# NSA units that hold one branch of two heads, and output projections that begin inside the attention, in a two-layer hybrid-attention kernel

## The chip, the cores and the metric

The kernel runs on one core of one Trainium2 chip. The metric is the device time of one execution in microseconds (us), the median of the runs shown. Engines are named as the profile names them: PE is TensorE's matmul, PEld its weight load, DVE is VectorE, ACT ScalarE, POOL GpSimd, SP SyncE (here the queue that issues the weight DMAs).

## What is computed

A forward pass over 256 tokens of width 1024 through two layers in fp32. Each layer is: half a SwiGLU feed-forward block, a mixer, half a feed-forward block, each with a norm that is scaled and shifted by a conditioning vector, and gated into the residual. Layer 0's mixer is the even one, layer 1's the odd one. Cut to what matters here:

```python
def even_mixer(y, ...):
    # 8 MLA heads: causal softmax attention, q and k of 96 columns, v of 64
    o_a = mla_mixer(...)
    # 8 NSA heads in 2 groups; k and v are shared by the 4 heads of a group
    o_b = gt[0] * o_c + gt[1] * o_s + gt[2] * o_w   # compressed, selected, window branch
    return concat([o_a, o_b]) @ w_out               # [256, 1024] @ [1024, 1024]

def odd_mixer(y, ...):
    o_c = dilated_mixer(...)    # 4 slots, each one softmax over 3 groups of heads
    o_d = moba_mixer(...)       # 4 heads
    return concat([o_c, o_d]) @ w_out               # [256, 512] @ [512, 1024]
```

With 256 tokens the selected branch covers every block and the window covers every key, so both are a causal softmax over 256 keys with a bias, each with its own k, v and gate. The compressed branch is 15 keys a head.

## The kernel before

**Exact products.** A dense product with weights is done as three fp32r matmuls of 512 columns (`mm3`, lines 198 to 200): high part times high part, high times the weights' low part, low times high. Each weight piece of 128 x 1024 therefore is prepared first: `prep` copies the DMA's slot to H on ACT (line 161) and, deferred, subtracts it to L on DVE (line 166). At most four pieces are prepared ahead (`HLN`); `piece(i)` hands out the i-th of them and issues subtractions still owed, `settle` issues all that are owed, `pop` gives the first one back and prepares the next. Slots come by SP's queue, eight at a time, and the next DMA is issued when a slot is done with.

**Attention.** `attention` runs over units in a software pipeline; each engine gets its instructions in the order of the code. In step i (lag 2), with `fill(i)` at its end:

```python
s3(i - 3)        # even i: values of a pair of units, PE L1107, into one PSUM bank o
turns(i - 2)     # probabilities transposed, PE L1080
s0(i + 2)        # scores, PE L1025 and L1026, then warm[i + 2] warming products, PE L479
scale(i - 1)     # DVE L1067 to L1072
logits(i + 1)    # bias, mask and row minimum, DVE L1037 and L1039
exps(i)          # ACT L1052
s4()             # o split in a high and a low part, ACT L832 and DVE L833
out_of(i - 2)    # the transposes copied to PT, ACT L1090 (a third branch: DVE L1088)
settle(); fill(i)
```

The even mixer has 16 units: 0 to 7 are the MLA heads, 8 to 15 the NSA heads, one unit a head, in the order (p, g) with head 4g + p. An NSA unit has two branches, selected and window. q and k of group g lie in partitions 64g to 64g + 63, so both branches of a unit use the same half of the partitions for their scores, which have 64 rows. `s3` takes two units and writes their 64 output columns to the two halves of o; it goes over branches, then over key tiles z, then over the two units. For NSA the pair starts with one product for the compressed branch (`extra`, PE L1553). `WKE` and `WKO` give the warming products of each unit in the even and the odd attention; a warming product is a matmul of the identity whose result is not used. `fill` runs background work: two products of the next conditioning vector (DVE L497), in steps 1 to 9 the compressed branch's chain, and from step 13 on `prep(True)` for the first pieces of the output projection. The odd mixer has 8 units, even ones with three branches in one softmax, odd ones with one.

**PSUM.** Two tags with four banks each: `acc` for transposes, o and projections, `wps` for scores and the transposes of the next norm.

**Output projection.** `out_proj` runs behind the attention and a flush of the background work: 8 pieces j times 2 token tiles t times 6 products in the even mixer, 4 pieces in the odd one. `oT` holds the rows of the MLA heads (j 0 to 3), `o2` those of the NSA heads (j 4 to 7). Behind tile 0's last product the residual and the norm of tile 0 (`blk.res(0)`) run on DVE and ACT while PE does tile 1; then `blk.tr(0)` transposes tile 0 for the next feed-forward block (PE L695).

Of the kernel before, what the change touches and what calls it, by code (L numbers as in the profile page):

```python
# [27 lines left out]
HLN = 4  # L28
# [8 lines left out]
def kernel(  # L37
# [572 lines left out]
    WKO = 4, 0, 0, 6, 2, 4, 2, 4  # L610
    WKE = 2, 1, 2, 2, 2, 2, 2, 2, 1, 1, 2, 2, 2, 1, 1, 1
# [402 lines left out]
    def attention(ap, units, stile, lag, fill, warm):  # L1014

        n = len(units)
        nbmax = max(len(u["br"]) for u in units)
        st = {}

        def s0(i):  # L1020
            u = units[i]
            st[i] = []
            for qT, kT, _, _ in u["br"]:
                ps = wps()
# [68 lines left out]
        def s3(i):  # L1093
            pair = [(units[j], st.pop(j), j % 2) for j in (i - 1, i)]
            o = acc()
# [4 lines left out]
            for b in range(nbmax):  # L1100
                for z in range(2):
                    for u, pt, hp in pair:
                        nb = len(u["br"])
                        if b >= nb:
                            continue
                        v = u["br"][b][3]
                        T.matmul(o[64 * hp:64 * hp + 64, 128 * z:256], lhsT=v[z], rhs=pt[:, b, 256 * z:256 + 128 * z],  # L1107
                                 start=first and b == 0 and z == 0, stop=b == nb - 1 and z == 1,
                                 skip_group_check=True)
# [33 lines left out]
    def out_proj(oT, nj, n):  # L1143
        o = [[acc(), acc()] for _ in range(2)]
        blk = Block(o, n)

        def mm(t, j, h, l, qr=(0, 1)):
            tsl = slice(128 * t, 128 * t + 128)
            sh, sl = oT(j)
            for q in qr:  # L1150
                qs = slice(512 * q, 512 * q + 512)
                mm3(o[t][q], sh[:, tsl], sl[:, tsl], h[:, qs], l[:, qs], j == 0, j == nj - 1)

        for j in range(nj - HLN):
            for t in range(2):
                mm(t, j, *piece(0))
            pop()
        for t in range(2):
            for j in range(HLN - QM):
                mm(t, nj - HLN + j, *piece(0 if t else j))  # L1160
                if t:
                    pop(later=True)
            for q in range(2):
                for j in range(QM):
                    mm(t, nj - QM + j, *piece((0 if q else j) if t else HLN - QM + j), qr=(q,))
                    if t and j < QM - 1 and q:
                        pop(later=True)
            if t:
                settle(LS)
                blk.tr(0)  # L1170
                pop(later=True)
# [780 lines left out]
```

## Time and profile before

| what | value |
|---|---|
| median of 3 runs | 1102.04 us (1101.65 to 1104.19) |
| profiled execution, its own time | 1103.17 us |
| span of the profiled execution | 1101.4 us |
| mean granted PE clock | 0.987 of full |
| PE busy | 1049.4 us, 95% of the span |
| DVE busy | 828.2 us, 75% |
| ACT busy | 533.5 us, 48% |
| DMA | 250.77 MB, 228 GB/s over the span |

The times in the rows are from the span's start. The even mixer's attention starts its first scores at 306.8 us and its last values end at 370.7; its projection ends at 392.9. The odd attention's first scores start at 855.4, and its projection runs from 890.8 to 902.0. A busy share is an average over all stages; what a change in one stage is worth is read from the stage itself, from the waits that end last there. Matmuls are pipelined, so their own durations are longer than the distance from one to the next.

### The profile page before, as it was taken

What the parts mean: (1) busy time and instruction counts of PE and PEld (TensorE: products, weight loads), DVE (VectorE), ACT (ScalarE), POOL (GpSimd) and SP (SyncE); (2) the same over time, 40 slices, a digit from 0 to 9 for tenths busy, and PEclk for the clock granted to TensorE, in tenths of its full rate; (3) what the DMA queues carried; (4) which work ended last, traced back from release to release, by engine and by line L of the source; (5) the groups of instructions that cost most, each with busy time, mean ns of one, the idle gap of its engine ahead of it and who ended that gap; (6) DMA issues with size and microseconds to landing.
All of it is one profiled execution on the core that took longest, in us unless ns stands there. A gap on an engine that the chain in (4) does not pass through costs nothing.

```text
span 1101.4 us, 14077 instructions
## 1 busy us (share of the span) xinstructions
PE 1049.4 (95%) x5031; PEld 847.6 (77%) x5031; DVE 828.2 (75%) x1430; ACT 533.5 (48%) x913; POOL 45.9 (4%) x93
## 2 busy tenths in 40 slices
PE   6899999997989989999999999999999999999998
PEld 5678778876677768888887888888688777888886
DVE  5779877769788488997757999864779868666653
ACT  4444434554348466444446544433645666444441
POOL 3000020003400000000000000000000000000000
PEclk9999999999989999999999999999999999999999
DMA  9999998747690357999863899884278517765500
GB/s 335 306 364 339 317 347 258 259 142 248 224 243 2 115 177 244 353 363 304 269 209 115 270 357 344 283 286 151 77 253 244 153 39 262 234 229 191 164 1 38
DMA packets 169818, 250.77 MB, mean 228 GB/s; under 512 B 10741, under 2 KB 111559, under 8 KB 169748
## 3 DMA queue, kind: packets, MB, share of 16 engines
q1 hardware_dynamic: 166736, 248.35, 68.8%
q0 software_dynamic: 2576, 1.39, 0.9%
q8 instruction: 39, 0.64, 0.3%
q14 instruction: 31, 0.25, 0.1%
q10 hardware_dynamic: 436, 0.13, 0.0%
HBM read 247.59 MB, written 2.23 MB: 227 GB/s over the span
## 4 chain that ended last, share of the span: by engine, by line
PE 79%; DVE 10%; ACT 4%; DMA 3%; issue 2%; SPq 1%; POOL 0%; ACTq 0%; DVEq 0%
PE wps L198 13%; PE wps L200 13%; PE wps L199 13%; PE acc L198 10%; PE acc L200 10%; PE acc L199 10%; DVE L L166 3%; DMA slot<-in_ada_w_dram 2%; PE wps L880 2%; DVE ada L497 2%; PE acc L1107 1%; ACT xn L1052 1%; ACT H L161 1%; DMA slot<-in_ffn_w_in_dram 1%; SPq L95 1%
## 5 line engine op out<-in xcount | busy, mean ns | idle before, releaser
L166 DVE TENSOR_TENSOR L<-slot,H 128x1024 fp32r<-128x1024 f32 (+4 forms) x316 | 376.7, 1200 | 136.3 <-ACT H L161 128.5
L161 ACT ACTIVATE H<-slot 128x1024 fp32r<-128x1024 f32 (+4 forms) x316 | 325.7, 1040 | 280.5 <-PE acc L200 134.5
L198 PE MATMUL wps<-H,y 128*128 128x512 f32 (+1 forms) x736 | 290.2, 394 | 1.7 <-ACT y L714 1.6
L199 PE MATMUL wps<-L,y 128*128 128x512 f32 (+1 forms) x736 | 285.2, 387 | 6.3 <-DVE L L166 4.6
L200 PE MATMUL wps<-H,y 128*128 128x512 f32 (+1 forms) x736 | 284.8, 387 | 0.0
L199 PEld LDWEIGHTS wps<-L,y 128*128 128x128 f32 x736 | 139.2, 189 | 36.2 <-DVE L L166 10.9
L198 PEld LDWEIGHTS wps<-H,y 128*128 128x128 f32 x736 | 139.1, 189 | 28.8 <-ACT y L714 1.8
L200 PEld LDWEIGHTS wps<-H,y 128*128 128x128 f32 x736 | 138.8, 189 | 28.4 <-DVE y L720 0.9
L198 PE MATMUL acc<-H,gT 128*128 128x512 f32 x352 | 142.5, 405 | 1.0 <-DVE g L868 1.0
L200 PE MATMUL acc<-H,gT 128*128 128x512 f32 x352 | 138.5, 393 | 0.0
L199 PE MATMUL acc<-L,gT 128*128 128x512 f32 x352 | 138.2, 393 | 0.0
L497 DVE SCALAR_TENSOR_TENSOR ada<-slot,c,ada 128x512 f32<-128x512 f32 x155 | 116.3, 751 | 2.9
L198 PEld LDWEIGHTS acc<-H,gT 128*128 128x128 f32 x352 | 66.0, 188 | 24.7 <-issue 11.0
L200 PEld LDWEIGHTS acc<-H,gT 128*128 128x128 f32 x352 | 66.0, 188 | 15.4
L497 DVE SCALAR_TENSOR_TENSOR ada<-slot,cact,ada 128x512 f32<-128x512 f32 x96 | 72.1, 751 | 5.6 <-DMA slot<-in_ada_w_dram 3.8
L199 PEld LDWEIGHTS acc<-L,gT 128*128 128x128 f32 x352 | 66.1, 188 | 13.3
L832 ACT ACTIVATE gT<-wps 128x512 fp32r<-128x512 f32 (+2 forms) x53 | 26.5, 501 | 94.6 <-PE wps L880 90.5
L866 ACT ACTIVATE s<-wps 128x256 f32<-128x256 f32 (+1 forms) x86 | 31.9, 377 | 47.0 <-PE wps L200 46.4
L198 PE MATMUL acc<-H,y 128*128 128x512 f32 (+2 forms) x128 | 50.1, 392 | 2.2 <-ACT H L161 1.1
L199 PE MATMUL acc<-L,y 128*128 128x512 f32 (+2 forms) x128 | 49.4, 386 | 2.7 <-DVE L L166 2.7
L833 DVE TENSOR_TENSOR gT<-wps,gT 128x512 fp32r<-128x512 f32 (+2 forms) x53 | 30.1, 568 | 27.6 <-ACT gT L832 26.8
L200 PE MATMUL acc<-H,y 128*128 128x512 f32 (+2 forms) x128 | 49.2, 384 | 0.1
(333 smaller groups left out, 1037.4 us busy)
## 6 DMA issues: line engine op xcount, KB each, us to landing
slot<-in_ffn_w_in_dram SPq DMA_DIRECT2D x160, 512.0 KB, 6.3
slot<-in_ffn_w_out_dram SPq DMA_DIRECT2D x40, 1024.0 KB, 7.0
slot<-in_ada_w_dram SPq DMA_DIRECT2D x160, 256.0 KB, 5.4
slot<-in_ada_w_dram SPq DMA_DIRECT2D x24, 1024.0 KB, 7.3
slot<-in_od_w_in_dram SPq DMA_DIRECT2D x12, 1024.0 KB, 5.2
slot<-in_ada_w_dram SPq DMA_DIRECT2D x16, 512.0 KB, 9.6
slot<-in_ffn_w_in_dram SPq DMA_DIRECT2D x16, 384.0 KB, 4.3
slot<-in_nsa_cmp_w_dram SPq DMA_DIRECT2D x4, 1024.0 KB, 9.2
```

What stands on the lines that cost most here:

```text
L95: nc.sync.dma_start(view(t), src)
L161: A.activation(hv, w, AF.Copy)
L166: eng.tensor_tensor(lv, w, hv.bitcast(F32), op=OP.subtract)
L198: T.matmul(o, lhsT=sh, rhs=wh, start=start, stop=False)
L199: T.matmul(o, lhsT=sh, rhs=wl, start=False, stop=False)
L200: T.matmul(o, lhsT=sl, rhs=wh, start=False, stop=stop)
L497: V.scalar_tensor_tensor(a, w[:, j], c[:, j:j + 1], a, op0=OP.mult, op1=OP.add)
L832: A.activation(dst[0], src, AF.Copy)
L833: V.tensor_tensor(dst[1], src, dst[0].bitcast(F32), op=OP.subtract)
L866: A.activation(s[:, 0:m], ab[t][:, 0:m], AF.Silu)
L880: T.transpose(ps[0:mm, 256 * ft + 128 * t:256 * ft + 128 * t + 128], st[u, t][:, 128 * ft:128 * ft + mm], ident)
L1052: A.activation(s[b][:, c0:c1], s[b][:, c0:c1], AF.Exp, scale=-1.0, bias=nm[:, b, q:q + 1], accum_out=den[:, b, q:q + 1])
```

## The change

NSA units are regrouped: a unit is now one branch b of the two heads p and 4 + p, of which one lies in partitions 0 to 63 and the other in 64 to 127. A pair of units still holds the same two heads and both branches. `s3` then goes over the pair's first unit and its second unit one after another, and alternates between the two heads inside a unit.

`out_proj` becomes a class. `begin` swaps the two PSUM tags, so that the projection's four accumulators take the banks of the scores, and `some` issues blocks (t, j) of 6 products in `fill`: in the even attention 8 of 16 blocks in steps 14 to 18 (`EF`), in the odd one 3 of 8 in steps 7 to 9 (`OF`). `end` issues the rest in the order of before. Pieces 0 to 3 of the even projection are given back inside the attention, and each time the next one is prepared; the first preparation moves from step 13 to step 12. The warming products are fewer: MLA units have 1 each (15 before, 8 now), NSA units none (11 before), the last two odd units none (6 before).

```diff
+    sets = ["a", "w"]
+    def bank_of(tag):
+        return psum.tile([128, 512], F32, tag=tag, name={"a": "acc", "w": "wps"}[tag])
     def acc():
-        return psum.tile([128, 512], F32, tag="acc", name="acc")
+        return bank_of(sets[0])
     def wps():
-        return psum.tile([128, 512], F32, tag="w", name="wps")
+        return bank_of(sets[1])
...
-    WKO = 4, 0, 0, 6, 2, 4, 2, 4
-    WKE = 2, 1, 2, 2, 2, 2, 2, 2, 1, 1, 2, 2, 2, 1, 1, 1
+    WKO = 4, 0, 0, 6, 2, 4, 0, 0
+    WKE = 1, 1, 1, 1, 1, 1, 1, 1, 0, 0, 0, 0, 0, 0, 0, 0
+    EF = {14: ((0, 0),), 15: ((1, 0), (0, 1)), 16: ((1, 1), (0, 2)), 17: ((1, 2), (0, 3)), 18: ((1, 3),)}
+    OF = {7: ((0, 0),), 8: ((0, 1),), 9: ((0, 2),)}
...
+        mine, scores = [lambda tag=tag: bank_of(tag) for tag in sets]
...
             for qT, kT, _, _ in u["br"]:
-                ps = wps()
+                ps = scores()
...
-                ps = acc()
+                ps = mine()
...
-            for b in range(nbmax):
+            if "both" in units[i]:
+                steps = [(u, pt, b, b, j == 0, j == 1) for u, pt, j in pair for b in range(2)]
+                steps = [steps[0:2], steps[2:4]]
+            else:
+                steps = [[(u, pt, b, hp, b == 0, b == len(u["br"]) - 1) for u, pt, hp in pair if b < len(u["br"])]
+                         for b in range(nbmax)]
+            for group in steps:
                 for z in range(2):
-                    for u, pt, hp in pair:
-                        nb = len(u["br"])
-                        if b >= nb:
-                            continue
+                    for u, pt, b, hp, begin, end in group:
                         v = u["br"][b][3]
                         T.matmul(o[64 * hp:64 * hp + 64, 128 * z:256], lhsT=v[z], rhs=pt[:, b, 256 * z:256 + 128 * z],
...
-    def out_proj(oT, nj, n):
-        o = [[acc(), acc()] for _ in range(2)]
-        blk = Block(o, n)
...
+    class OutProj:
+        def begin(self):
+            sets.reverse()
+            self.o = [[acc(), acc()] for _ in range(2)]
...
+        def some(self, *tj):
+            for t, j in tj:
+                gone = sum((z, i) in self.made for i in range(self.nj - HLN) for z in (1,))
+                self.mm(t, j, *piece(j - gone))
+                self.made.add((t, j))
+                if t and j < self.nj - HLN:
+                    pop(later=True)
+
+        def end(self):
+            nj, made = self.nj, self.made
+            blk = Block(self.o, self.n)
+            self.some(*[(t, j) for j in range(nj - HLN) for t in range(2) if (t, j) not in made])
+            for t in range(2):
+                for j in range(HLN - QM):
+                    if (t, nj - HLN + j) not in made:
+                        self.mm(t, nj - HLN + j, *piece(0 if t else j))
+                    if t:
+                        pop(later=True)
...
-                    if i >= 13:
+                    if i >= 12:
                         prep(True)
+                    if i == 14:
+                        proj_out.begin()
+                    proj_out.some(*EF.get(i, ()))
...
-                def mk2(p, g):
-                    h = 4 * g + p
-
+                def mk2(p, b):
...
-                    gs = slice(64 * g, 64 * g + 64)
-                    return dict(br=[(qT[gs, p, :], kT[gs, b, :], ba[:, h, :],
-                                     [vn[t][:, b, 64 * g:64 * g + 64] for t in range(2)]) for b in range(2)],
-                                extra=extra_, gate=gv[:, h, 1:3, :], dst=lambda: dst2(p))
+                    br = []
+                    for g in range(2):
+                        gs = slice(64 * g, 64 * g + 64)
+                        br.append((qT[gs, p, :], kT[gs, b, :], ba[:, 4 * g + p, :],
+                                   [vn[t][:, b, 64 * g:64 * g + 64] for t in range(2)]))
+                    return dict(br=br, both=True, extra=extra_, gate=gv[:, p:8:4, 1 + b, :], dst=lambda: dst2(p))
...
-                attention(e2, units + [mk2(p, g) for p in range(4) for g in range(2)], ring, 2, fill, WKE)
+                proj_out = OutProj(lambda j: (oT[:, j, 0], oT[:, j, 1]) if j < 4 else
+                                   (o2[0][:, j - 4, 0], o2[0][:, j - 4, 1]), 8, 1)
+                attention(e2, units + [mk2(p, b) for p in range(4) for b in range(2)], ring, 2, fill, WKE)
                 bg_flush()
...
+                return proj_out.end()
...
                     bg(QA[i])
+                    if i == 6:
+                        proj_out.begin()
+                    proj_out.some(*OF.get(i, ()))
+
+                proj_out = OutProj(lambda j: (oT[:, j, 0], oT[:, j, 1]), 4, 4)
                 attention(o2, units, ring, 2, fill, WKO)
```

## Rows read from the trace of the kernel before

**Rows 1.** The page, part 4: the shares of the chain that ended last, by engine.

```profile
PE 79%; DVE 10%; ACT 4%; DMA 3%; issue 2%; SPq 1%; POOL 0%; ACTq 0%; DVEq 0%
```

**Rows 2.** Windows: the busy time of each engine by stage. Columns: stretch in us, its length, busy time and instructions of PE, PEld, DVE, ACT and POOL, the granted PE clock, the DMA engines' busy share, GB/s. The stages are the half-clock stretch of the MLA units, two NSA stretches, the end of the even attention, its projection, the end of the odd attention, its projection.

```profile
316.30:324.40 8.10, 8.10 (x43) 7.09 (x43) 4.77 (x19) 3.92 (x14) 1.01 (x2) 0.62 1.13 258
...
332.50:345.40 12.90, 12.90 (x83) 9.64 (x83) 12.39 (x63) 10.23 (x39) 0.00 (x0) 1.00 0.00 1
345.40:357.28 11.88, 11.88 (x80) 8.72 (x80) 9.92 (x57) 10.07 (x38) 0.00 (x0) 1.00 0.01 2
357.28:370.70 13.42, 11.59 (x77) 7.74 (x77) 8.23 (x20) 9.57 (x27) 0.00 (x0) 0.87 0.26 79
370.70:392.94 22.24, 22.24 (x98) 18.21 (x99) 11.06 (x19) 8.58 (x12) 0.00 (x0) 1.00 0.43 142
...
877.40:890.78 13.38, 11.90 (x84) 8.39 (x84) 9.12 (x36) 7.66 (x26) 0.00 (x0) 1.00 0.21 78
890.78:901.98 11.20, 11.20 (x50) 8.98 (x50) 6.09 (x15) 4.61 (x8) 0.00 (x0) 1.00 0.01 2
```

**Rows 3.** The chain that ended last, in order of time, in the NSA steps of the even attention. Columns: start us, us, engine, output, line, how many instructions (a matmul of fp32 operands is two).

```profile
346.43 0.64 PE wps L479 x4
...
350.09 1.45 PE acc L1107 x16
351.54 0.81 PE acc L1080 x6
352.34 0.41 PE wps L1025 x2
352.76 0.43 PE wps L1026 x2
353.19 0.22 PE wps L1025 x2
353.41 0.43 PE wps L1026 x2
353.85 0.42 PE wps L479 x2
354.27 0.66 PE acc L1080 x6
...
356.84 0.43 PE acc L1553 x2
```

**Rows 4.** All waits of DVE from 324 to 357.3 us (us in total, times, longest), and the row of the timeline with the longer one (idle time before it and what ended it in brackets).

```profile
DVE yb L833 <- ACT yb L832: 1.6, 1, 1.6
DVE qTn L828 <- PE acc L1444: 0.7, 1, 0.7
...
352.00 0.42 DVE L833 TENSOR_TENSOR yb<-acc,yb 128x256 fp32r<-128x256 f32 x1 [1.63 <-ACT yb L832]
```

**Rows 5.** The timeline of ACT in steps 12 and 13: the split of a pair, the two PT copies of unit 11 and the first H copy of the projection's pieces.

```profile
351.58 0.39 ACT L832 ACTIVATE yb<-acc 128x256 fp32r<-128x256 f32 x1 [1.48 <-PE acc L1107]
...
354.69 0.87 ACT L1090 ACTIVATE PT<-acc 128x384 f32<-128x384 f32 x2
...
355.45 1.06 ACT L161 ACTIVATE H<-slot 128x1024 fp32r<-128x1024 f32 x1
```

**Rows 6.** The chain again, at the end of the even attention and where the next stage's transposes begin.

```profile
361.12 1.74 ACT xn L1052 x8
362.86 0.38 ACT PT L1090
...
363.29 2.72 PE acc L1107 x11
...
392.94 0.89 PE wps L695 x8
```

**Rows 7.** Windows again, columns as in rows 2: stretches around the two falls of the PE clock in the even attention, and a stretch of the odd attention with little PE work.

```profile
314.00:316.30 2.30, 0.00 (x1) 0.01 (x1) 2.16 (x7) 0.00 (x0) 0.54 (x1) 0.86 1.09 346
...
316.00:318.00 2.00, 1.70 (x7) 1.52 (x8) 1.93 (x5) 0.81 (x3) 1.01 (x2) 0.50 1.09 348
...
359.22:363.29 4.07, 2.29 (x14) 1.20 (x12) 4.00 (x10) 3.99 (x13) 0.00 (x0) 1.00 0.01 2
...
364.00:366.00 2.00, 2.00 (x12) 1.20 (x9) 0.54 (x3) 0.56 (x1) 0.00 (x0) 0.50 0.73 173
...
880.60:884.39 3.79, 2.31 (x15) 1.45 (x14) 3.27 (x14) 3.79 (x17) 0.00 (x0) 1.00 0.55 199
```

**Rows 8.** The chain at the end of the odd attention, and from the timeline there a joint pair's values and the transposes of unit 5.

```profile
882.07 0.27 ACT oTo L832
...
883.97 0.38 ACT PT L1090
...
886.13 1.66 PE acc L1080 x12
...
890.11 0.66 PE wps L583 x2
...
901.98 0.89 PE wps L695 x8
...
878.50 2.16 PE L1107 MATMUL acc<-PT,vt 128*64 128x256 f32 x16
...
882.77 0.55 PE L1080 MATMUL acc<-cp,xn 128*128 128x128 f32 x3 [0.98 <-ACT PT L1090]
```

More of the change, by code (lines that the diff above doesn't have):

```diff
@@ L1094, in s3 @@
             pair = [(units[j], st.pop(j), j % 2) for j in (i - 1, i)]
-            o = acc()
+            o = mine()
             first = True
@@ L1099, in s3 @@
                 first = False
-            for b in range(nbmax):
+            if "both" in units[i]:
[5 more added lines that the diff above has]
+            for group in steps:
                 for z in range(2):
-                    for u, pt, hp in pair:
-                        nb = len(u["br"])
-                        if b >= nb:
-                            continue
+                    for u, pt, b, hp, begin, end in group:
                         v = u["br"][b][3]
                         T.matmul(o[64 * hp:64 * hp + 64, 128 * z:256], lhsT=v[z], rhs=pt[:, b, 256 * z:256 + 128 * z],
-                                 start=first and b == 0 and z == 0, stop=b == nb - 1 and z == 1,
-                                 skip_group_check=True)
+                                 start=first and begin and z == 0, stop=end and z == 1, skip_group_check=True)
             st["o"] = (units[i]["dst"], o)
@@ L1150, in mm @@
             for q in qr:
                 qs = slice(512 * q, 512 * q + 512)
-                mm3(o[t][q], sh[:, tsl], sl[:, tsl], h[:, qs], l[:, qs], j == 0, j == nj - 1)
-        for j in range(nj - HLN):
-            for t in range(2):
[L1156 to L1160, printed above, removed]
+                mm3(self.o[t][q], sh[:, tsl], sl[:, tsl], h[:, qs], l[:, qs], j == 0, j == self.nj - 1)
@@ new lines, in some @@
+        def some(self, *tj):
[9 more added lines that the diff above has]
+            self.some(*[(t, j) for j in range(nj - HLN) for t in range(2) if (t, j) not in made])
+            for t in range(2):
+                for j in range(HLN - QM):
[3 more added lines that the diff above has]
+                        pop(later=True)
+                for q in range(2):
+                    for j in range(QM):
+                        if (t, nj - QM + j) not in made:
+                            self.mm(t, nj - QM + j, *piece((0 if q else j) if t else HLN - QM + j), qr=(q,))
+                        if t and j < QM - 1 and q:
+                            pop(later=True)
@@ L1161, in out_proj @@
                 if t:
+                    settle(LS)
+                    blk.tr(0)
                     pop(later=True)
[L1163 to L1171, printed above, removed]
-            else:
-                blk.res(0)
@@ L1174, in out_proj @@
-        return blk
+                else:
+                    blk.res(0)
+            return blk
     def load_bias(dst, b0, eng):
```

11 lines of the change are left out of this document (6 added, 5 removed).

## The prediction, made blind

> **What bounds the kernel now.** I read the page first: the chain that ended last is 79% TensorE [rows 1], and nearly all of it is the dense products of lines 198 to 200, which the change moves but does not thin. So only the two attention stages and the products right behind them can move. I then read the windows by stage [rows 2]. The reader is to see that TensorE is busy without a gap in both NSA stretches and in both projections, that the two stretches in which it is not, 357.28 to 370.70 and 877.40 to 890.78, are the ends of the two attentions, and that DMA stands still from 332.5 to 357.28, so no transfer is late there.
>
> Next the chain through the NSA steps [rows 3]: every link is TensorE, one step's scores 0.41 + 0.43 + 0.22 + 0.43 = 1.49 us, warming products 0.42 (one) or 0.64 (two), six transposes 0.66 to 0.81, the compressed branch's product 0.43, the values 1.45. But VectorE is as tight: between 324 and 357.3 it waits twice only, 0.7 us on the copy of q and 1.63 us at 352.00 on the split of a finished pair [rows 4]. So from 324.4 to 350.4 a faster TensorE buys nothing, and what it can buy first is that 1.63 us. ScalarE comes third: 1.74 us of exponentials, 0.87 for two PT copies, 0.39 for the split, 1.06 for each H copy [rows 5, 6].
>
> The end of the even attention is read from the same chain [rows 6]: the exponentials and a PT copy on ScalarE hold TensorE until 363.29, and then the values take 2.72 us for 11 passes. [...]
>
> **Scores in two halves.** The values show how halves behave: 16 passes in 1.45 us [rows 3]. At 0.215 a pass of 256 columns and 0.11 of 128 they would be 8 x 0.215 + 8 x 0.11 = 2.6 us one after another, so two output halves run at once. For scores the order in the queue stays head 0 (128, 256 columns), head 1 (128, 256). If matmuls start in order, head 1's first passes can begin only beside the last 256-column pass of head 0, which saves 0.22 a unit. Bounds: 0 if row halves don't overlap, 0.65 if a whole head disappears. I take 0.22, since the values' passes too overlap in order: 8 units, 1.8 us of TensorE.
>
> **Warming products.** Each costs 0.22 (0.64 less 0.42). NSA units lose 11 (2.4 us), MLA units 7 (1.5 us), odd units 6 (1.3 us). In the odd attention and behind 324.4 in the even one they are hidden: ScalarE and VectorE carry the odd chain until 884.35 [rows 8], VectorE the even one until 350.4. Two MLA units lie in 316.3 to 324.4, where the clock is 0.62 and TensorE is busy all 8.10 us [rows 2] and ahead of VectorE's 0.7 us wait; one product there is 0.43 at the low clock, one 0.22: I take 0.5 us, bounds 0 and 0.65.
>
> The rows show the clock low after 2.30 us with no matmul (314 to 316.3, then 0.50), but full through 2.31 busy of 3.79 us in the odd attention [rows 7]. With 4.2 us taken from the 24.8 us between 332.5 and 357.28, TensorE still works for 20.6 of them, so I count no loss. [...]
>
> **Order of the values.** A unit now holds one branch of two heads, so the first half of a pair's values (0.73 of 1.45) needs only the first unit's PT; before, each branch alternated between both units. That half runs ahead of the wait.
>
> **Preparation one step earlier.** H copy and L subtraction of weight piece 0 move from step 13 to step 12, and pieces 4 to 7 from the projection into steps 15 to 18. VectorE has room for the L's: 8.23 busy of 13.42 us at the end [rows 2]. ScalarE gets 1.06 more before unit 11's PT. No DMA is added; the slots only come free earlier, and the queues are empty then.
>
> **The even sum.** Unit 11's PT was ready at 354.69 + 0.87 = 355.56 [rows 5]. It moves by -0.5 (MLA), -1.63 (VectorE's wait, since values of units 8 and 9 now start on their PT and not behind 2.4 + 1.8 us of scores and warming), +1.06 (H copy): 354.5. With 0.73 of the values ahead of it, TensorE's list starts as if at 353.8 where it started at 357.28. From there it has no gaps. A block is 6 products: 96 took 22.24 us (98 records in that window, two of them the next stage's) [rows 2], so 0.232 each and 1.39 a block. The list, with 0.2 for each drain between products and narrower passes not yet in the rows (two of them):
> three pairs of values 3 x 1.45; two compressed products 2 x 0.63 with their drain; four sets of transposes 0.81 + 0.66 + 0.81 + 0.66; eight blocks 11.1; the 48 products left 11.1; drains 0.4. Sum 4.35 + 1.26 + 2.94 + 11.1 + 11.1 + 0.4 = 31.2, so the next stage's transposes start at 385.0 and not at 392.94 [rows 6]: 7.9 us gained.
> Does anything else bind? ScalarE from 354.5 to unit 13's PT: H 1.06, exponentials 1.74, split 0.39, PT 0.87, H 1.06, exponentials 1.74, PT 0.87 = 7.7, at 362.2. TensorE needs that PT at 353.8 + 1.45 + 0.81 + 1.39 + 0.66 + 2.78 + 0.63 + 0.73 = 362.25. They meet; if ScalarE is later, the blocks' cover is gone and each us there costs one. Banks: the blocks' four were the score banks, free after unit 15's logits, which is before 357.28 less the shift.
>
> **The odd sum.** The wait before unit 5's transposes is for a bank that the split of the pair before frees, behind the exponentials [rows 8]: not touched. Block 1 runs 883.3 to 884.7, where unit 5's PT came at 884.35; then values 2.1, twelve transposes 1.66, two blocks 2.8, values 2.1, the gate's product 0.66, 30 products at 0.233 = 7.0: 901.1, where the transposes started at 901.98 [rows 8]. Gain 0.9; bounds -0.6 (three more drains) and 2.0 (all of TensorE's idle time there: 13.38 less 11.90 [rows 2], and the rest of the warming).
>
> **Sum.** 7.9 + 0.9 = 8.8 us. The profiled execution has a span of 1101.4 and took 1103.17; less 8.8 it is 1094.4. The median of the three runs is 1102.04, 1.13 below it: 1093.2.
>
> **Rivals.**
> 1. Only the gaps at the ends are filled; the start of the list stays at 357.28 because VectorE or ScalarE, saturated in the steps before, don't let it move. Then 392.94 - 357.28 = 35.66 against 31.2: 4.5, plus 0.9: 1096.6. For it: ScalarE was busy 10.07 of 11.88 us in 345.4 to 357.28 [rows 2] and gets an H copy more. Against: VectorE's 1.63 us wait is real, and it waited for TensorE.
> 2. The clock falls in the NSA steps, for want of warming products, and the kernel is slower. [...] For it: the fall at 364 came in the same stage. Against: the odd row named above.
> 3. The change doesn't do what it says: the blocks stand in TensorE's queue ahead of transposes and values that ScalarE waits for, and stretch the attention by what they take off the projection. Then the gain is the idle time that remains, near 0: 1102. Against: in steps 16 to 18 no exponentials are left, so little waits.
> 4. All of TensorE's savings count, as if VectorE were not tight: 4.2 + 0.65 + 0.73 before the list, then 4.5 and 2.0: 12.1 us, 1089.9. Against: VectorE's two waits sum to 2.3 us.
>
> **How the numbers follow.** Forecast (gains 6 to 11 us) 0.63, rival 1 (3.5 to 6) 0.18, rival 3 0.08, rival 2 0.07, rival 4 0.04. The measurement can tell about 0.3%, 3.3 us. Faster: 0.63 + 0.18 + 0.04 = 0.85; same 0.08; slower 0.07. The range goes from rival 4 to the weakest of rival 1 (a gain of 3.5): 1090 to 1098.5, which leaves out 0.15 above and a little below; the forecast's own range is 1091 to 1096.
>
> **What would show it.** Right: L479 gone from the NSA steps; unit scores at 1.27 and not 1.49; VectorE's wait on the pair of units 8 and 9 under 0.5 us; lines 198 to 200 between the transposes from about 357 on, with the clock at 1.00; the next transposes (L695) near 385 and 8.8 us earlier after the odd stage. Wrong: a clock under 0.9 between 330 and 370; TensorE waiting for PT between blocks; a second wait of VectorE of over 1 us; FFN stages of another length than before.

## The result, and the profile after

The changed kernel took 1093.65 us (median of 8 runs, 1090.37 to 1096.28) where the kernel before took 1103.24 on the same chip (8 runs): a ratio of 0.9913, interval 0.9895 to 0.9931. That is 9.6 us faster; the forecast was 1093.2 us, 8.8 us below before. The profiled execution of after has a span of 1092.4 and took 1094.18, 9.0 us less than that of before on either count.

Five marks split both spans into stages: the first transposes of the MLA heads, the first product with the compressed keys (kcT), the next stage's transposes behind the even projection, the copy of k at the start of the odd attention, and the next transposes behind the odd projection.

| stretch, us | before | after | less | forecast |
|---|---|---|---|---|
| start to MLA transposes | 302.95 | 303.64 | -0.69 | 0 |
| MLA units, to kcT | 26.40 | 26.19 | 0.21 | 0.5 |
| NSA units and even projection | 63.43 | 53.89 | 9.54 | 7.4 |
| feed-forward stages, to copy of k | 464.50 | 464.47 | 0.03 | 0 |
| odd attention and projection | 44.54 | 44.71 | -0.17 | 0.9 |
| rest | 199.58 | 199.50 | 0.08 | 0 |

So that the total came out near the forecast is in part luck, out of errors that cancel: the even stage (MLA, NSA and projection) gave 9.75 for 7.9, the odd one, in this execution, nothing for 0.9, and the stages ahead took 0.69 longer.

The page of after, parts 1 and 4: busy times, and the chain by engine (before: [rows 1]).

```profile
PE 1038.4 (95%) x4983; PEld 837.6 (77%) x4983; DVE 827.3 (76%) x1430; ACT 532.5 (49%) x913; POOL 45.9 (4%) x93
...
PE 76%; DVE 13%; ACT 4%; DMA 4%; issue 2%; POOL 0%; SPq 0%; ACTq 0%; DVEq 0%
```

TensorE lost 3% of the chain, VectorE gained 3: the NSA steps are no longer a chain of TensorE links [rows 3] but of VectorE's, up to 351.2. Windows of after: MLA units, NSA units up to the gapless list, that list, and the odd stage (columns as in [rows 2]).

```profile
303.64:329.83 26.19, 22.06 (x143) 18.76 (x142) 21.93 (x76) 13.18 (x42) 2.07 (x4) 0.87 1.02 253
329.83:353.34 23.51, 23.48 (x172) 15.82 (x172) 22.67 (x120) 19.81 (x74) 0.00 (x0) 1.00 0.01 3
353.34:383.72 30.38, 30.29 (x169) 23.81 (x166) 21.09 (x53) 18.84 (x43) 0.00 (x0) 1.00 0.44 139
848.19:892.90 44.71, 41.42 (x248) 31.68 (x247) 31.82 (x127) 26.91 (x91) 0.00 (x0) 0.96 0.38 111
```

The list of TensorE work is whole (30.29 us busy of 30.38) and at a clock of 1.00 from 353.34 on; below full clock are the MLA units (0.87) and the odd stage (0.96). The chain of after at the start and end of the list:

```profile
350.50 0.34 DVE xn L1049
350.85 0.34 DVE yb L841
351.28 1.84 ACT xn L1062 x8
353.12 0.38 ACT PT L1100
353.55 1.24 PE acc L1120 x7
354.79 0.81 PE acc L1090 x6
355.60 0.23 PE wps L204
...
383.88 0.89 PE acc L703 x8
```

The seven records at 353.55 are the second half of a pair's values; the first half ran ahead of the wait, so the list counts from 354.79 - 1.45 = 353.34. From there to 383.88 it has no gap: 30.54 us, where before took 35.66 from 357.28 to 392.94.

Scores on TensorE, from the timeline of after. The queue holds head 0 (128 columns, 256), then head 1 (128, 256).

```profile
349.43 0.50 PE L1035 MATMUL wps<-kTn,qTn 64*128 64x128 f32 x4
349.75 0.61 PE L1036 MATMUL wps<-kTn,qTn 64*128 64x256 f32 x4
350.29 0.88 PE L1090 MATMUL acc<-cp,xn 128*128 128x128 f32 x6
```

Both heads' 128-column passes are recorded ahead of both heads' 256-column ones (the four records of the first start by 349.7, the first of the others at 349.75), and the four products of a unit are over in 350.29 - 349.43 = 0.86 us, against 1.49 [rows 3]. Five of the eight NSA units show this; in the other three the second head starts later and the unit takes 1.30 to 1.65 us up to the next instruction.

### The profile page after: what moved, and what is told of

It is laid out like the page before. It is cut to its first block, busy times and chain, and to the rows that moved or that the text cites. A ratio compares the mean times of both kernels' runs of the same rounds, so it can differ in the third digit from the quotient of the medians.

```text
span 1092.4 us, 13983 instructions
## 1 busy us (share of the span) xinstructions
PE 1038.4 (95%) x4983; PEld 837.6 (77%) x4983; DVE 827.3 (76%) x1430; ACT 532.5 (49%) x913; POOL 45.9 (4%) x93
## 4 chain that ended last, share of the span: by engine, by line
PE 76%; DVE 13%; ACT 4%; DMA 4%; issue 2%; POOL 0%; SPq 0%; ACTq 0%; DVEq 0%
PE wps L204 12%; PE wps L206 12%; PE wps L205 12%; PE acc L204 11%; PE acc L206 11%; PE acc L205 11%; DVE L L172 3%; DMA slot<-in_ffn_w_in_dram 2%; DVE ada L503 2%; DMA slot<-in_ada_w_dram 1%; ACT xn L1062 1%; ACT H L167 1%; PE wps L888 1%; DVE xn L1049 1%; PE acc L888 1%
## 5 line engine op out<-in xcount | busy, mean ns | idle before, releaser
L205 PE MATMUL wps<-L,y 128*128 128x512 f32 (+1 forms) x448 | 174.4, 389 | 5.6 <-DVE L L172 4.7
L204 PE MATMUL wps<-H,y 128*128 128x512 f32 (+1 forms) x448 | 177.3, 396 | 1.7 <-ACT y L1835 1.6
L206 PE MATMUL wps<-H,y 128*128 128x512 f32 (+1 forms) x448 | 173.7, 388 | 0.0
L204 PE MATMUL acc<-H,y 128*128 128x512 f32 (+2 forms) x416 | 162.5, 391 | 3.5 <-ACT y L722 1.6
L205 PE MATMUL acc<-L,y 128*128 128x512 f32 (+2 forms) x416 | 159.6, 384 | 4.0 <-DVE L L172 4.0
L206 PE MATMUL acc<-H,y 128*128 128x512 f32 (+2 forms) x416 | 159.7, 384 | 0.1
L204 PEld LDWEIGHTS wps<-H,y 128*128 128x128 f32 x448 | 84.9, 190 | 19.4 <-ACT y L1835 2.0
L206 PEld LDWEIGHTS wps<-H,y 128*128 128x128 f32 x448 | 84.7, 189 | 17.4 <-DVE y L728 0.4
L205 PEld LDWEIGHTS acc<-L,y 128*128 128x128 f32 x416 | 78.2, 188 | 19.4 <-DVE L L172 5.9
L204 PEld LDWEIGHTS acc<-H,y 128*128 128x128 f32 x416 | 78.2, 188 | 18.2 <-ACT y L722 1.8
L206 PEld LDWEIGHTS acc<-H,y 128*128 128x128 f32 x416 | 78.1, 188 | 15.7 <-DVE y L728 0.9
L204 PE MATMUL acc<-H,gT 128*128 128x512 f32 (+1 forms) x176 | 71.3, 405 | 1.0 <-DVE g L876 1.0
L204 PE MATMUL wps<-H,gT 128*128 128x512 f32 (+1 forms) x176 | 71.2, 404 | 0.0
L206 PE MATMUL acc<-H,gT 128*128 128x512 f32 (+1 forms) x176 | 69.3, 394 | 0.0
L205 PE MATMUL acc<-L,gT 128*128 128x512 f32 (+1 forms) x176 | 69.2, 393 | 0.0
L206 PE MATMUL wps<-H,gT 128*128 128x512 f32 (+1 forms) x176 | 69.1, 393 | 0.0
```

The costliest lines, as they stand in the source:

```text
L204: T.matmul(o, lhsT=sh, rhs=wh, start=start, stop=False)
L205: T.matmul(o, lhsT=sh, rhs=wl, start=False, stop=False)
L206: T.matmul(o, lhsT=sl, rhs=wh, start=False, stop=stop)
```

## The experiments

Eleven runs follow: ten edits of the changed kernel, and that kernel once more. Each is read by the stages above, since stages whose code is the same in all of them (from the start to the MLA units, the feed-forward stages, the rest) differ between executions by up to 3.5 us (the start takes 302.95 to 306.42), and the clock with them. For instance the rest is 201.14 and not 199.50 us where this window of the run with the odd warming products shows a fall; in after the same stretch stays at 1.00:

```profile
908.00:910.00 2.00, 2.00 (x9) 1.81 (x8) 1.56 (x5) 0.78 (x3) 0.00 (x0) 0.50 0.97 219
```

The stretch from kcT to the next transposes ("NSA stretch" below) repeats better: with its code unchanged and the clock at 1.00 in it, it took 53.86 to 53.90 us in five executions, after's among them. In two runs of the table the clock fell at its start, to 0.50 from 334 to 336 us (values alternate) and from 330 to 332 us (gate warm), so these two are to be read with that.

| run | us, median | MLA | NSA stretch | odd |
|---|---|---|---|---|
| before | 1103.24 | 26.40 | 63.43 | 44.54 |
| after | 1093.65 | 26.19 | 53.89 | 44.71 |
| after again | 1094.45 | 25.53 | 53.86 | 43.45 |
| no early blocks | 1100.47 | 26.00 | 57.86 | 46.07 |
| old units | 1098.59 | 26.05 | 55.30 | 44.90 |
| old warming | 1094.32 | 26.40 | 53.87 | 43.47 |
| odd warming | 1093.73 | 26.06 | 53.88 | 43.46 |
| odd step 6 | 1092.04 | 25.85 | 53.90 | 42.11 |
| MLA warm | 1094.82 | 25.75 | 53.89 | 43.46 |
| preparation at 13 | 1098.51 | 26.25 | 57.34 | 44.73 |
| scores interleaved | 1094.14 | 25.86 | 53.89 | 44.13 |
| gate warm | 1089.93 | 23.25 | 54.10 | 42.08 |
| values alternate | 1095.14 | 24.77 | 54.76 | 43.45 |

**No early blocks.** All products of both projections behind the attentions again, everything else as in after.

```diff
-    EF = {14: ((0, 0),), 15: ((1, 0), (0, 1)), 16: ((1, 1), (0, 2)), 17: ((1, 2), (0, 3)), 18: ((1, 3),)}
-    OF = {7: ((0, 0),), 8: ((0, 1),), 9: ((0, 2),)}
+    EF = {}
+    OF = {}
```

> The changed kernel with all blocks of both output projections behind the attention (units, warming products and preparation as changed). Theory (the blocks fill TensorE's idle time and keep its clock up at the ends of the attentions): the projection of the even mixer starts about 6 us later than its last 48 products could, the clock falls again to 0.50 between unit 13's PT and the end, and the even stretch (80.2 us in the changed kernel, from the MLA transposes to the next block's transposes) is 85.5 to 87; the odd one changes by less than 1.5 us. Time 1099 to 1101. Rival (most of the gain comes from the NSA steps before, the blocks only displace other work): even stretch 80 to 82, time 1093 to 1095.

1100.47 us, ratio 0.9962 (0.9931 to 0.9992). The NSA stretch is 57.86, so the blocks are worth 3.97 us there; the odd stage is 1.4 longer than in after, each with the clock at 0.50 in its trace (880 to 882 here, 874 to 876 in after); the other parts, without them, 63.43 - 57.86 = 5.57. The even stage came out at 83.9, between what theory and rival said: blocks and the rest share the gain. The theory's fall of the clock didn't come: it is 1.00 from 357 to 387, so here the blocks fill idle time and no more. Its timeline shows what the blocks fill:

```profile
357.85 0.87 PE L1120 MATMUL acc<-PT,vn 128*64 128x256 f32 x8
360.29 1.24 PE L1120 MATMUL acc<-PT,vn 128*64 128x256 f32 x8 [1.57 <-ACT PT L1100]
```

The first half of a pair's values does run ahead, and then TensorE still waits 1.57 us for the second PT; ahead of the transposes before them it waited 1.14 us for another PT copy.

**Old units.** A unit holds both branches of one head again, so both heads of a unit use the same half of the rows and values alternate between the units; the blocks stay.

```diff
-                def mk2(p, b):
+                def mk2(p, g):
...
-                    return dict(br=br, both=True, extra=extra_, gate=gv[:, p:8:4, 1 + b, :], dst=lambda: dst2(p))
+                    gs = slice(64 * g, 64 * g + 64)
+                    return dict(br=[(qT[gs, p, :], kT[gs, b, :], ba[:, h, :],
+                                     [vn[t][:, b, 64 * g:64 * g + 64] for t in range(2)]) for b in range(2)],
+                                extra=extra_, gate=gv[:, h, 1:3, :], dst=lambda: dst2(p))
```

> The changed kernel with NSA units of one head and two branches, as before. Theory: a unit's scores take 1.27 to 1.49 us again and never 0.86, the values of units 10 and 11 wait for both PT, and the gapless list starts 1 to 1.5 us later; even stretch 81.2 to 81.7, time 1094.6 to 1095.2. Rival 1 (VectorE bounds the NSA steps and the regrouping is worth nothing): even stretch 80.0 to 80.5, time 1093.6. Rival 2 (the regrouping carries the whole earlier start of the list, 3.5 us and more): time 1097 or above.

1098.59 us, ratio 0.9959 (0.9941 to 0.9976); the NSA stretch is 55.30, 1.41 more than in after, as the theory said. The total alone would speak for the second rival; in the profiled execution the rest of the loss lies in untouched stages, 1.5 us in the start, where the clock in its records is 0.83 from 40 to 50 us and 1.00 in after, and 1.5 in the feed-forward stages. Unit 11's PT copies start 23.89 us behind kcT, 0.70 later than in after (23.19). In the timeline the scores stand in the queue's order and take 1.49:

```profile
354.12 0.48 PE L1035 MATMUL wps<-kTn,qTn 64*128 64x128 f32 x2
354.45 0.59 PE L1036 MATMUL wps<-kTn,qTn 64*128 64x256 f32 x2
354.88 0.38 PE L1035 MATMUL wps<-kTn,qTn 64*128 64x128 f32 x2
355.10 0.59 PE L1036 MATMUL wps<-kTn,qTn 64*128 64x256 f32 x2
```

**Values alternate.** The new units, but a pair's values in the order of before.

```diff
-                steps = [steps[0:2], steps[2:4]]
+                steps = [[steps[0], steps[3]], [steps[2], steps[1]]]
+                steps = [[(u, pt, b, hp, z == 0, z == 1) for u, pt, b, hp, _, _ in g] for z, g in enumerate(steps)]
```

> Against the changed kernel: the same units and scores, but a pair's values in the order of before, one head of each unit in turn, so that the first half needs the second unit's PT as well. Theory (the prediction's 0.73 us: the half that runs ahead of the wait for unit 11's PT is on the path): even stage 80.08 -> 80.7 to 80.9. Rival (the list has slack there, or the scores' halves alone give what the run with the old units lost, 1.27 us): 79.8 to 80.2.

1095.14 us, ratio 0.9920 (0.9889 to 0.9950). The even stage as a whole is 79.53, below what either said, since the MLA units took 24.77 us where after's took 26.19. The NSA stretch, in which the edit lies, is 54.76, 0.87 more than in after. But not all of that is the edit. The clock fell ahead of it, where after has 1.00:

```profile
334.00:336.00 2.00, 2.00 (x13) 1.39 (x11) 1.46 (x5) 0.88 (x2) 0.00 (x0) 0.50 0.03 8
```

The PT copies of units 8 and 11 in this run, and those of unit 8 in after (unit 11 there: 353.02):

```profile
345.81 0.85 ACT L1100 ACTIVATE PT<-acc 128x384 f32<-128x384 f32 x2
...
354.80 0.85 ACT L1100 ACTIVATE PT<-acc 128x384 f32<-128x384 f32 x2
```

```profile
344.03 0.85 ACT L1100 ACTIVATE PT<-acc 128x384 f32<-128x384 f32 x2
```

Unit 8's, which stand ahead of the first values that the edit touches, start 345.81 - 331.19 = 14.62 us behind kcT, in after 344.03 - 329.83 = 14.20; unit 11's 23.61 and 23.19. So 0.42 of the 0.87 was there before the edit, and 0.45 is left for the order of the values, less than the theory's 0.73. If the two parts add, the scores in two halves gave the other 0.96 of the 1.41; 0.70 of it shows as the later PT in the run with the old units.

**Scores interleaved.** Both heads' 128 columns queued first, then both heads' 256.

```diff
-            for qT, kT, _, _ in u["br"]:
-                ps = scores()
+            st[i] = [scores() for _ in u["br"]]
+            for ps, (qT, kT, _, _) in zip(st[i], u["br"]):
                 T.matmul(ps[:, 0:128], lhsT=qT[:, 0:128], rhs=kT[:, 0:128], start=True, stop=True)
+            for ps, (qT, kT, _, _) in zip(st[i], u["br"]):
                 T.matmul(ps[:, 128:384], lhsT=qT[:, 128:256], rhs=kT[:, 0:256], start=True, stop=True)
-                st[i].append(ps)
```

> Against the changed kernel: the scores of the two heads are queued as 128 columns of both, then 256 columns of both, where the changed kernel queues head 0 (128, 256) and then head 1 (128, 256). Theory (matmuls of the other half of the array's rows start ahead of their turn, so the order within a unit is nothing): the scores of a unit with both banks free take 0.86 us as now, even stage 79.8 to 80.4. Rival (matmuls start in the order of the queue and the 0.86 is a mistake of the records): scores shorter by 0.2 us or more a unit than with the old order, and up to 1 us less for the even stage.

1094.14 us, ratio 0.9897 (0.9845 to 0.9950); the NSA stretch is 53.89, to the hundredth that of after, and the records are the same:

```profile
349.96 0.49 PE L1035 MATMUL wps<-kTn,qTn 64*128 64x128 f32 x4
350.28 0.60 PE L1037 MATMUL wps<-kTn,qTn 64*128 64x256 f32 x4
```

So this order in the queue within a unit was worth nothing here: with the order of after, too, the second head's 128-column products were recorded ahead of the first head's 256-column ones, which the queue has before them (by 349.7 and from 349.75 on, above). In the odd attention, which shares this code, the three heads of a unit use the same half of the rows, and there the order cost something: with the clock at 1.00 the stage took 44.13 us, 0.68 more than in after's second execution below. By its trace the first unit's third head, whose 128 columns now stand ahead of the others' 256, waits 0.43 us for ScalarE's copy of k, and unit 5's transposes come 26.14 us behind VectorE's copy of k where that execution has 25.49; no run tests this cause by itself.

**Preparation at 13.** The H copy and L subtraction of weight piece 0 in step 13 again, and those of the next pieces a step later each.

```diff
-                    if i >= 12:
+                    if i >= 13:
```

> Against the changed kernel: the H copy and the L subtraction of weight piece 0 stand in step 13 again, as before the change. Theory (in step 12 the copy ran while ScalarE waited for logits of unit 13 anyway, so the 1.06 us that the prediction charged cost nearly nothing): even stage 79.7 to 80.5. Rival (the prediction's: the copy is ahead of unit 13's exponentials and costs 1.06 us on the path): 78.9 to 79.2.

Both were wrong: the NSA stretch became 57.34, 3.45 longer (1098.51 us, ratio 0.9928, 0.9899 to 0.9956). First VectorE, then TensorE, then the clock:

```profile
357.62 1.21 DVE L172 TENSOR_TENSOR L<-slot,H 128x1024 fp32r<-128x1024 f32 x1
```

```profile
355.97 0.48 PE L204 MATMUL wps<-H,oT 128*128 128x512 f32 x1
358.89 0.75 PE L205 MATMUL wps<-L,oT 128*128 128x512 f32 x1 [2.44 <-DVE L L172]
```

```profile
357.00:359.00 2.00, 0.11 (x1) 0.11 (x1) 1.97 (x8) 2.00 (x5) 0.00 (x0) 0.99 0.00 0
359.00:361.00 2.00, 2.00 (x5) 1.56 (x6) 1.97 (x6) 1.64 (x8) 0.00 (x0) 0.50 0.00 0
```

One step later the L of piece 0 stands behind another unit's scaling and logits on a VectorE that is busy 1.97 of each 2.00 us. The first block stops after one product for 2.44 us, the transposes behind it stop too, and the clock then is 0.50 from 359 to 361. The same run prices the copy itself: without it unit 11's PT copies start 353.38 - 331.12 = 22.26 us behind kcT, in after 353.02 - 329.83 = 23.19. So the copy in step 12 costs 0.93 on the path, near the rival's 1.06, and the stretch is 3.45 longer without it all the same.

**Old warming** and **odd warming.** The old counts of warming products everywhere (WKE as before too), and in the odd attention alone.

```diff
-    WKO = 4, 0, 0, 6, 2, 4, 0, 0
+    WKO = 4, 0, 0, 6, 2, 4, 2, 4
```

> The changed kernel with the warming products of before in both attentions. Theory (they cost TensorE 0.22 us each, hidden behind VectorE but for some): even stretch 0.5 to 2 us longer, the odd stretch 0.8 to 1.3 us shorter since its clock no longer falls; time 1093.0 to 1094.5. Rival (they are what keeps the clock up, and taking them away cost something in the even attention too): even stretch no longer than 80.2, time under 1093.

> The changed kernel with the warming products of the last two odd units put back (2 and 4). Theory (without them TensorE sat idle for 2.56 us before unit 5's transposes, its clock fell to 0.50, and the first block took 0.43 us a product where it takes 0.23): clock 1.00 through the odd attention, first block 1.4 us, odd stretch 43.6 to 44.0 where the changed kernel has 44.9; time 1092.3 to 1092.9. Rival (the odd blocks delay the values whatever the clock): odd stretch 44.6 to 45, time 1093.6.

1094.32 us (ratio 0.9923, 0.9900 to 0.9947) and 1093.73 (0.9919, 0.9895 to 0.9943). The NSA stretch is 53.87 and 53.88: with the new units in place, the old products in the NSA units cost nothing and gave nothing, and the first theory's 0.5 to 2 us were not there. In the odd stage both came out at 43.46 to 43.47, a little under the second theory's 43.6, with the clock at 1.00 and a wait of 0.98 us before unit 5's transposes where after has 2.56. That the products kept the clock up isn't shown by this: the next run has the same time and clock without them.

**MLA warm.** Eight warming products instead of one behind MLA unit 2.

```diff
-    WKE = 1, 1, 1, 1, 1, 1, 1, 1, 0, 0, 0, 0, 0, 0, 0, 0
+    WKE = 1, 1, 8, 1, 1, 1, 1, 1, 0, 0, 0, 0, 0, 0, 0, 0
```

> Against the changed kernel: eight warming products instead of one behind MLA unit 2, so that TensorE works through its 2.3 us without a matmul at 314 to 316.3, after which the granted clock was 0.66, 0.50, 0.50 and 0.63 in the four stretches from 316 to 324. Theory (these units run at half clock because of that gap, and TensorE sets their pace): clock 0.9 or more from 316 to 324, even stage (first MLA transposes to the next stage's transposes) 80.08 -> 77 to 78.6. Rival (VectorE sets the pace behind it anyway, as the prediction said of the steps behind 324.4; the whole prediction gave the MLA units only 0.5 us and 0.21 came): 79.6 to 80.3, with the clock up all the same.

1094.82 us, ratio 0.9902 (0.9866 to 0.9939): it tells nothing of the MLA units, since the products ran ahead of the gap and not in it, and the clock fell all the same (0.50 from 316 to 322).

```profile
310.12 1.95 PE L485 MATMUL wps<-cp 128*128 128x128 f32 x16
...
316.79 0.79 PE L589 MATMUL wps<-ahl,onesr 128*128 128x512 f32 x1 [1.82 <-DVE ahl L581]
```

But its odd stage, whose code is that of after, took 43.46 with the clock at 1.00.

**After again.** The changed kernel, nothing edited.

> The changed kernel once more, nothing edited. In its first trace the clock fell to 0.50 at 874 in the odd stage, behind 2.56 us without a matmul; in the run with more warming products in the MLA units the odd stage had the same code and the same 2.56 us, and the clock stayed at 1.00 (odd stage 43.46 and not 44.71). Theory (whether the clock falls behind such a gap hangs on when it comes, and is fixed for a program only as far as its timing repeats): odd stage is either 44.7 with the fall or 43.4 to 43.5 without, nothing between, even stage 79.6 to 80.3. Rival (something in the program itself sets it): 44.7 with the fall again.

1094.45 us (7 runs; before 1103.28 on that chip; ratio 0.9913, 0.9881 to 0.9944). The odd stage took 43.45. Unit 5's transposes and the clock around them, first in the trace of after:

```profile
873.68 0.90 PE L1090 MATMUL wps<-cp,xn 128*128 128x128 f32 x3 [2.56 <-ACT PT L1100]
```

```profile
872.00:874.00 2.00, 0.32 (x2) 0.32 (x3) 1.58 (x8) 2.00 (x10) 0.00 (x0) 0.75 0.52 123
874.00:876.00 2.00, 2.00 (x7) 1.70 (x6) 1.74 (x6) 1.77 (x7) 0.00 (x0) 0.50 0.97 397
```

and in the second execution:

```profile
874.12 0.55 PE L1090 MATMUL wps<-cp,xn 128*128 128x128 f32 x3 [2.56 <-ACT PT L1100]
```

```profile
872.00:874.00 2.00, 0.00 (x0) 0.00 (x0) 1.55 (x9) 2.00 (x10) 0.00 (x0) 1.00 0.29 37
874.00:876.00 2.00, 1.88 (x11) 1.34 (x11) 1.93 (x6) 2.00 (x8) 0.00 (x0) 1.00 0.97 381
```

The same program, the same 2.56 us without a matmul: once the clock falls to 0.50 and the stage takes 1.26 us more, once it stays at 1.00. So the odd stage's missing gain in the first trace is a fall of the clock that comes in some executions. Of the eight traces in which this wait is 2.48 to 2.56 us, three show the clock at 0.50 behind it (after from 874 to 876, no early blocks from 880 to 882, preparation at 13 from 878 to 880), four stay at 1.00 (after again, scores interleaved, MLA warm, values alternate), and in the eighth, old units, the stage is as long as with a fall (44.90). What decides between the two these traces don't show, so the theory's cause stays open.

**Odd step 6.** Two blocks in the odd step 6, where TensorE has its 2.56 us.

```diff
-    OF = {7: ((0, 0),), 8: ((0, 1),), 9: ((0, 2),)}
+    OF = {6: ((0, 0), (1, 0)), 7: ((0, 1),), 9: ((0, 2),)}
```

> Against the changed kernel: in the odd attention the products of two blocks stand in step 6 instead of one in step 7, so they run in the 2.56 us in which TensorE waits for unit 5's PT (871.1 to 873.7), where now the clock falls to 0.50. Theory (the fall of the clock, not the missing cover, is what the odd stage lost, and the idle time is worth filling besides): granted clock 1.00 in the whole stretch 866 to 893, products at 0.23 each, odd stage (copy of k to the next stage's transposes) 44.71 -> 42.3 to 42.8, whole kernel about 1091.4. Rival A (only the clock matters): 43.4 to 43.6, as with the warming products put back. Rival B (the blocks in step 6 delay the transposes of unit 5 and those keep ScalarE waiting, so the gain is lost behind them): 44.3 or more.

1092.04 us, ratio 0.9878 (0.9838 to 0.9917). The odd stage is 42.11 with the clock at 1.00, 1.34 less than in after's second execution and a little under the theory's 42.3. Twelve products now stand where the gap was (2.8 us), but not all of it comes out at the end: TensorE finishes early and waits for the normalisation.

```profile
890.61 1.06 PE L703 MATMUL wps<-cp,xn 128*128 128x128 f32 x8 [1.04 <-DVE xn L691]
```

**Gate warm.** Odd step 6, and twelve warming products right ahead of the gate's two products in the MLA units, where in after TensorE waited 3.04 us for VectorE and the clock then was 0.50 from 318 to 322.

```diff
+            keep_warm(ps, gate_warm[0])
             for z in range(2):
                 T.matmul(ps, lhsT=onesr, rhs=st[1 + z], start=z == 0, stop=z == 1)
...
+    GW = 0, 1
...
+                    gate_warm[0] = 12 if i in GW else 0
                     bg(PA[i])
+                    gate_warm[0] = 0
```

> Two edits to the changed kernel in stages that don't touch: the two blocks in the odd step 6 (as in the run with them alone), and twelve warming products in TensorE's queue right ahead of the gate's two products in the MLA units, where it then waits 3.04 us for VectorE (313.9 to 317.1). Theory (the half clock of the MLA units comes from that wait, and TensorE sets the pace behind it, as VectorE's waits of 1.43, 0.67 and 0.77 us there say): clock 0.9 or more from 316 to 324, even stage 80.08 -> 77 to 78; odd stage 42.1 again; whole kernel about 1089.5. Rival (VectorE catches up its waits in the steps behind 324, so the faster clock is worth nothing at the end): clock up, even stage 79.6 to 80.3, whole kernel about 1092.

1089.93 us, ratio 0.9868 (0.9828 to 0.9909), the lowest median of all, though its interval overlaps that of odd step 6. This time the products fill the gap, and the clock stays up:

```profile
312.88 2.92 PE L485 MATMUL wps<-cp 128*128 128x128 f32 x24
...
316.89 0.51 PE L592 MATMUL wps<-ahl,onesr 128*128 128x512 f32 x1 [0.85 <-DVE ahl L583]
```

```profile
318.00:320.00 2.00, 2.00 (x20) 1.70 (x19) 1.96 (x9) 1.78 (x7) 0.20 (x1) 1.00 1.11 337
320.00:322.00 2.00, 2.00 (x17) 1.78 (x15) 1.86 (x10) 1.62 (x8) 0.00 (x0) 1.00 1.15 194
```

In after the same units show, over the same stretch:

```profile
318.00:320.00 2.00, 2.00 (x9) 1.82 (x8) 1.70 (x8) 1.84 (x6) 0.44 (x1) 0.50 1.11 348
320.00:322.00 2.00, 2.00 (x13) 1.67 (x12) 0.75 (x1) 0.41 (x1) 0.00 (x0) 0.50 1.15 196
```

The MLA units take 23.25 us, for 26.19 and 25.53 in the two executions of after and 24.77 to 26.25 in all nine with that code: 1.5 to 3.0 us less. The NSA stretch behind them is 0.2 longer, and there the clock, now full from 316 to 324, is 0.50 from 330 to 332. VectorE's busy time in 320 to 322 went from 0.75 to 1.86: in after it had been waiting for products of a TensorE at half clock, 1.43 us at the longest, and here it has no such wait.

```profile
321.16 0.75 DVE L836 TENSOR_SCALAR qTn<-acc,vec 128x512 f32<-128x512 f32 x1 [1.43 <-PE acc L1475]
```

The feed-forward stages of this trace are 1.36 longer than after's, with the clock at 0.85 from 780 to 790, so its time has about that much in it that the edits don't cause.

## Why the prediction was right or wrong

**The list behind the attention: right, but it was put 1.15 us too late.** Forecast was a list without gaps from 353.8 that lasts 31.2. Measured, with after's 0.69 us of drift taken off, it starts as if at 352.65 and lasts 30.54. The blocks come to 0.23 a product as forecast (records of 0.39 us that start 0.23 apart). The 0.2 us for a drain was my estimate; in after the first product behind the last pair's values takes 0.43 us on the chain and the next ones 0.23. The 0.66 us too much in the length is mostly such time that I counted twice: the compressed product takes 0.43 and I gave it 0.63, and I added 0.4 for further drains.

**The step that failed: VectorE's 1.63 us as all that a faster TensorE can win.** The forecast had unit 11's PT 0.57 us earlier behind kcT (1.63 less 1.06 for the H copy). It came 25.34 - 23.19 = 2.15 earlier, and 25.34 - 22.26 = 3.08 in the run without the copy. What was late was ScalarE. It had waited 1.48 us for values of the pair [rows 5], and behind that stood the split, PT copies and then the exponentials: those began at 352.87 where VectorE had been idle, its logits done, since 352.00 - 1.63 = 350.37 [rows 4]. That is 2.5 us of lateness, not 1.63; I took the shorter of two waits that had the same cause. And the 1.48 was only the longest of ScalarE's waits for TensorE. From 330 to 358 us in before they sum to 3.9 us (total, times, longest):

```profile
ACT yb L832 <- PE acc L1107: 1.5, 1, 1.5
ACT oT L832 <- PE acc L1107: 1.5, 2, 0.8
...
ACT PT L1090 <- PE acc L1080: 0.5, 2, 0.3
ACT gate L584 <- PE wps L583: 0.4, 1, 0.4
```

In after one of them is left:

```profile
ACT oT L840 <- PE acc L1120: 0.8, 1, 0.8
```

So "from 324.4 to 350.4 a faster TensorE buys nothing" holds for VectorE and not for ScalarE, which fell behind in just those steps. VectorE's 1.63 is gone too (only the 0.8 us for the copy of q is left there), and ScalarE starts its exponentials at 351.26:

```profile
350.32 1.05 ACT L167 ACTIVATE H<-slot 128x1024 fp32r<-128x1024 f32 x1
351.26 0.40 ACT L1062 ACTIVATE xn<-xn,nm 128x128 f32<-128x128 f32 x1
...
353.02 0.86 ACT L1100 ACTIVATE PT<-acc 128x384 f32<-128x384 f32 x2
```

**What no single run divides.** Taken back one at a time, the blocks are worth 3.97 us, the new units 1.41, the NSA warming products 0.0: 5.4 of the 9.54. For the other 4.2 no run has old units and old warming products together. What the traces show is that either saving alone takes most of ScalarE's waits for TensorE away: 1.3 us of the 3.9 are left with the old units, 0.8 with the old warming. So each looks cheap when the other is there, and how the 4.2 splits stays open.

**The H copy in step 12: price right, purpose missed.** 1.06 was charged and 0.93 measured. That with the L a step later the first block stops for 2.44 us, with the clock at 0.50 from 359 to 361 behind it, was not in the sum, which took the blocks' pieces to be ready.

**Scores: 0.22 a unit was too little.** They take 0.86 us and not 1.27 in five of the eight units, close to the upper bound of 0.65 saved. "If matmuls start in order" was the condition that failed. Of the up to 8 x 0.63 = 5.0 us of TensorE that this frees, at most 0.96 reaches the end of the stage with the warming products gone, so the step was wrong by much and the sum by little.

**Order of the values: right in kind, too high in size** (0.73 forecast; 0.45 left of the measured 0.87 without the 0.42 that stands ahead of the edit).

**Warming products: hidden in the NSA units, as forecast** (0.0 by the run with the old counts, which has the new units). The 0.5 in the MLA units can't be told from the clock's own spread there: 26.19 and 25.53 in the two executions of after, 26.40 with the old counts.

**The odd stage: 0.9 was right without a fall of the clock, 44.54 - 43.45 = 1.09.** "No clock loss" was not: with the products gone the wait for unit 5's PT is 2.56 us long and not 0.98, and behind it the clock was 0.50 in the one execution of after and 1.00 in the other.

**The rivals.** The first (the list doesn't move) falls: it starts some 4.6 us earlier, and even without blocks the other parts gave 5.57. The second (a fall in the NSA steps) didn't come in after: 1.00 from 329.83 to 383.72. It is near, though: with the preparation one step later the clock was 0.50 from 359 to 361, and in values alternate and gate warm it was 0.50 at the start of the NSA stretch (334 to 336, 330 to 332), with 0.4 and 0.2 us of lateness there. That the kernel is slower by such a fall no run shows; in after's odd stage, where products at 0.50 start 0.43 us apart and at 1.00 0.23, the fall went with 1.26 us. The third (blocks displace and gain nothing) falls by the 3.97 and 1.4 us of the run without them. The fourth (every TensorE saving counts, 12.1 us) has the list start at 357.28 - 5.58 = 351.7, the forecast at 353.8; measured was 352.65, about halfway between. Against its mechanism stand the chain of after, which is VectorE's up to 351.2, and the old warming products, which cost 0.0.

Left open: what part of the spread of the totals, some 6 us in after's own eight runs, each fall of the clock makes. The two slowest (1096.2 and 1096.3 us) have the lowest mean clocks, 0.982 and 0.978, the two fastest (1090.4) 0.989; but only profiled executions show where it fell.

## What to carry to other kernels

Where one engine idles in a saturated stretch, look at the others that wait for the same cause: the price is the longest lateness, not the wait that is easiest to read. Two savings that end the same waits look worthless when they are taken back one at a time; one run must take back both. Work moved into another engine's gap brings its suppliers' deadlines with it; the blocks of products were worth 3.97 us with their operands prepared one step earlier, which cost 0.93; prepared later, with the blocks where they are, the stretch took 57.34, near the 57.86 without blocks. And measure an edit by the stage it lies in, bounded by marks, when the rest moves by more than the edit does, here by up to 3.5 us.

## What the runs showed of the hardware

Products in the two halves of the rows overlapped, in the two orders of the queue that ran: 0.86 us for two heads of 128 and 256 columns in five of the eight units of after, against 1.49 in one half. A gap of 2.56 us in TensorE's work was followed by a clock of 0.50 in one execution and of 1.00 in another, for the same program. Behind a gap of 3.04 us in the MLA units the clock was 0.50 from 318 to 322; with twelve products of no use in the gap it was 1.00 and the units took 1.5 to 3.0 us less, with eight products ahead of the gap it was 0.50 from 316 to 322 all the same.
